# Where the sums, the shared expert and a block's steps stand on the engines of a two-layer model

## The chip, the cores and the metric

One core of a Trainium2 chip runs the whole kernel in one launch. The metric is the device time of one execution in microseconds (us), as the median of several runs. The profiler records one execution apart from these. An instruction belongs to one engine: TensorE (PE in the profile) multiplies matrices, and its weight loads have a lane of their own (PEld); VectorE (DVE), ScalarE (ACT) and GpSimd (POOL) work element by element; SyncE (SP) issues the transfers of the weights.

## The reference, cut to what matters

The model has two layers on 256 tokens of 1024 values. A vector c modulates each layer: the sums below are `silu(c) @ w`.

```python
def ada(c, w, b, n):
    m = jax.nn.silu(c) @ w + b
    return [t[:, None, :] for t in jnp.split(m, n, axis=-1)]

def modulate(h, shift, scale):
    return h * (1 + scale) + shift
...
def moe(h, w_router, e_bias, w_gate, w_up, w_down, ws_gate, ws_up, ws_down):
    ...
    routed = grouped_experts(xt, eidx, w, w_gate, w_up, w_down)
    shared = swiglu(xt, ws_gate, ws_up, ws_down)
    return (routed + shared).reshape(B, S, D)
...
    for i in range(DEPTH):
        sh1, sc1, g1, sh2, sc2, g2 = ada(c, ada_w[i], ada_b[i], 6)
        h = modulate(rmsnorm(x, norm_mix[i]), sh1, sc1)
        if i < N_A_LAYERS:
            y = gmlp_mixer(h, a_w_in[i], a_b_in[i], a_ln_g[i], a_ln_b[i],
                           a_w_s[i], a_b_s[i], a_w_out[i])
        else:
            if kv is None:
                kv = shared_kv(x, c, kv_norm, kv_ada_w, kv_ada_b, kv_w_k, kv_w_v)
            j = i - N_A_LAYERS
            y = moba_mixer(h, b_w_q[j], b_w_o[j], kv[0], kv[1], kv[2])
        x = x + g1 * y
        h = modulate(rmsnorm(x, norm_ffn[i]), sh2, sc2)
        x = x + g2 * moe(h, moe_router[i], moe_bias[i], moe_w_gate[i], moe_w_up[i],
                         moe_w_down[i], sh_w_gate[i], sh_w_up[i], sh_w_down[i])
    return rmsnorm(x, final_norm)
```

Each token goes to 8 of 64 experts, and to the shared expert besides. All inputs are float32.

## The kernel before

All of it lies on one core, in this order: the first eight sums and the norm; the gMLP mixer of layer 0; routing and experts of layer 0; attention of layer 1 with its shared keys and values; routing and experts of layer 1; the final norm.

**Weights.** They arrive in tiles of 1 MB (`w`, 128 partitions x 8 x 256 values) on SP's queue, in the order in which the program fetches them, each as soon as one of 14 places in a pool is free. A place is free once the last instruction that reads its tile is done.

**The mixer and attention** are lists of steps on PE (48 in the mixer: 16 `Tok`, 16 `Feat`, 16 `Out`). `split` prepares the weights of a coming step: `high` casts the tile to a rounded copy on ACT, and `low` writes the difference (`scr<-w,scr`) on DVE, on POOL at every fourth step from 16 to 43 in the mixer; two casts and two low halves are also made before the mixer's first step. Between steps, `tick` takes instructions of the open sums, as many as the table `BUDGET` grants each engine.

**A sum** (class `Sum`, 56 of them) is 256 columns of `silu(c) @ w`: one tile `w`, in which row-block k is scaled by column k of `cs` (silu of c) and the eight blocks are added. Mode "v" does it with 8 instructions on DVE. Mode "q" does it with 8 scalings on ACT and 3 additions on POOL. `lighter` chooses the mode when a sum begins. In both modes `total` then sums over the partitions with two matmuls of one column (`wk<-onesf,w`), and `close` adds the bias into `adaT` or `kvT`.

**The prologue of an expert stage** ranks the experts (`order`), after which SP can fetch experts in that order (experts 0 and 1 are fetched ahead). It places the tokens (`slotT`, `slotU`), works out routing weights (`wsel`, `GT`, `gu`), and runs the whole first half of the shared expert: `shared_up` (32 matmuls of 256 columns) and `shared_act`. `gather` then picks the tokens of the first four blocks (`s` is the selection matrix, built on DVE from `slotU`). `gates` scales the shared expert's last weights.

**The expert stage** runs 55 blocks of up to 128 token places; `ORDER` is the table in which experts, by rank, come to the blocks and their tiles are fetched; -1 in it stands for `shared_down`. On PE a block b is: `gate_up` of b, `scatter` of b-2 (adds results to the output), `share`, `down` of b-1, `flip` (transpose of b's activation), `place`, and `gather` for the next group of four. At block `SHARED_AT`, which follows from the place of -1, comes `shared_down`. A group's selection is prepared by `prep`. Most blocks are narrow: 32 columns of weights in each of four quarters of PE's columns.

Of the kernel before, what the change touches and what calls it, by code (L numbers as in the profile page):

```python
# [33 lines left out]
QUIET = (2, 5)  # L34

# [7 lines left out]
BUDGET = ((1.0, 1.2, 2.5), (1.6, 1.2, 2.5), (0.6, 1.2, 2.5))  # L43
# [11 lines left out]
BUDGET1 = ((1.3, 1.2, 2.5),) * 3 + ((0.8, 0.2, 2),) + ((1.8, 1.6, 3.4),) * 2 + ((1.4, 1.5, 2.5),) * 2  # L55
# [124 lines left out]
def tile_model(ctx: ExitStack, tc: tile.TileContext, A: dict, out: bass.AP):  # L180
# [103 lines left out]
    G.memset(onesf, 1.0)  # L284
    ident = cst.tile([P, P], F32, name="ident")
# [26 lines left out]
    class Sum:  # L312
# [3 lines left out]

        def __init__(self, w, biasT, at, dstT, dst=None, mode="v"):
            self.w, self.biasT, self.at, self.dstT, self.dst, self.mode = w, biasT, at, dstT, dst, mode
            self.ops = {V: [], S: [], G: []}
# [18 lines left out]
        def begin(self):  # L338
            for e in (V, S, G):
                for _, f in self.ops[e]:  # L340
                    f()
                self.ops[e] = []

        def total(self, pt):

            for q in range(2):
                T.matmul(pt[:, q:q + 1], self.w[:, 0, q * P:(q + 1) * P], onesf[:, 0:1], start=True, stop=True)
# [140 lines left out]
    def split(steps, k, pool, turns=None):  # L488
# [17 lines left out]
    credit = {V: 0, S: 0, G: 0}  # L506

    def tick(tv, ts, tg):

        spread()  # L510
        for f in list(active):
            if not f.left(V, S, G):
                f.age = getattr(f, "age", 0) + 1
                if f.age > 2:
                    f.finish()
                    active.remove(f)
        for e, t in ((V, tv), (S, ts), (G, tg)):
            credit[e] = min(credit[e], 0) + t
            for f in active:
                while credit[e] > 0 and f.ops[e] and not (e is G and f.left(V, S)):  # L520
# [4 lines left out]
    def lighter():  # L525

        return "q" if sum(f.left(S) for f in active) < sum(f.left(V) for f in active) + 0.1 else "v"

    def pump(*engs):

        for e in engs:
            for f in active:
                if not (e is G and f.left(V, S)):
# [4 lines left out]
    def settle(n=99):  # L538

        fs = [f for f in active if not f.left(V, S, G)][:n]  # L540
# [68 lines left out]
    def moe(l, own, rw, first, rest):  # L609
# [42 lines left out]
        pump(G)  # L652
# [6 lines left out]
        rest("q")  # L659
# [23 lines left out]
        pump(G)  # L683

# [20 lines left out]
        def gates():  # L705

            for q in range(2):
                S.copy(gq[64 * q:64 * q + 64, :], g2[l][64 * q:64 * q + 64, 512 * q:512 * q + 512])
            for k, eng in enumerate((G, V)):
# [79 lines left out]
        settle()  # L789
        close()  # L790
# [3 lines left out]
        shared_up(16 - SH1)  # L794
        spread()
# [6 lines left out]
        rest(*"vqvqvq")  # L802

        wsel = om([P, 2, NE])
        wsum = om([P, 2], tag="t1", bufs=8)
        for tt in range(2):
            V.scalar_tensor_tensor(wsel[:, tt, :], cr[:, tt, :], -2.5e38, sc[:, tt, :], ALU.is_lt, ALU.mult,
                                   accum_out=wsum[:, tt:tt + 1])
        wrec = om([P, 2], tag="t1", bufs=8)
        V.reciprocal(wrec, wsum)  # L810
        for tt in range(2):
            V.tensor_scalar(wsel[:, tt, :], wsel[:, tt, :], wrec[:, tt:tt + 1], 2.5, ALU.mult, ALU.mult)
        pump(V, S, G)
        ready = all(f.dst is None for f in active)
        if ready:
            gates()
# [3 lines left out]
        settle(1)  # L820
        close()
        shared_up(4)
        pgt = wk((NE, 256))
        for tt in range(2):
            T.transpose(pgt[:, tt * P:(tt + 1) * P], wsel[:, tt, :], ident)
        settle()
        close()
        spread()
        if not ready:
            flush(lambda f: f.dst is not None)  # L830
            gates()
        GT = om([NE, 256], tag="GT", bufs=1)
        S.copy(GT, pgt)
        pgu = wk((P, 2, NU))
        for tt in range(2):
            T.matmul(pgu[:, tt, :], GT[:, tt * P:(tt + 1) * P], puf, start=True, stop=True)
        gu = om([P, 2, NU, 2], F32R, tag="gu", bufs=1)
        V.tensor_copy(gu[:, :, :, 0], pgu)
        V.tensor_tensor(gu[:, :, :, 1], pgu, gu[:, :, :, 0], ALU.subtract)
# [142 lines left out]
        shared_act(0)  # L982
        shared_act(1)
        for c in range(4):
            gather(0, c)
        share(0)
        prep(1)
# [40 lines left out]
        def run():  # L1028
# [7 lines left out]
            for b in range(nblk + 2):  # L1036
                g, j = divmod(b, 4)

                late = b >= nblk - 1
                if b == SHARED_AT:  # L1040
# [12 lines left out]
                if b == nblk - 1:  # L1053
                    ht[b] = flip(hd)
                    scatter(sts.pop(b - 1), ys.pop(b - 1))
                if b == nblk or b >= 1 and not late:
                    y = finish(b - 1)
                if b == nblk + 1:
                    warm(10)
                    scatter(sts.pop(b - 2), ys.pop(b - 2))  # L1060
                if b < nblk:
                    if not late:
                        ht[b] = flip(hd)
                    pp = place(groups[g][1][:, 2 * j:2 * j + 2, :].rearrange("e u i -> e (u i)"))
                    if g + 1 < ng:
# [9 lines left out]
                tick(1.6, 1.6, 4.2)  # L1075
# [63 lines left out]
    with phase("pb") as pool:  # L1139
# [25 lines left out]
        for i in range(8):  # L1165
            f = ada(0, i, load(A["wada"][0, i]), "q" if i in QUIET else "v")
# [28 lines left out]
        for q in range(2):  # L1195
            low(early[q], wi[0][:, 4 * q:4 * q + 4, :], G)
# [100 lines left out]
        for k in range(n + 16):  # L1297
            for at, x in BEGIN:
                if at == k:
                    begin(x, lighter())  # L1300
            if k in (2, 6, 10):
                fetch_bv(512 * (k + 2) // 4, 512)
            split(steps, k, pool, 4 if 16 <= k < 44 else None)
# [23 lines left out]
            tick(*((0, 1.2, 0) if 17 <= k < 20 or k > 45 else BUDGET[k // 16]))  # L1327
# [309 lines left out]
```

## Time and profile before

| | us |
|---|---|
| three runs | 1463.18, 1464.41, 1467.83 |
| median | 1464.41 |
| profiled execution | 1460.32 |
| its span | 1458.6 |
| PE busy in the span | 1352.2 (93%) |
| PE weight loads | 893.6 (61%) |
| DVE busy | 853.3 (58%) |
| ACT busy | 537.5 (37%) |
| POOL busy | 213.9 (15%) |

The profiled execution's own time is 1.7 us above its span. Busy times are those of one execution; matmuls overlap, and their ends are modelled. The trace lists an fp32 matmul of the program as two instructions on PE. The clock granted to TensorE is given as a share of full speed; its mean over the execution is 0.961. The share of transfers is the mean over 16 DMA engines.

### The profile page before, as it was taken

What the parts mean: (1) busy time and instruction counts of PE and PEld (TensorE: products, weight loads), DVE (VectorE), ACT (ScalarE), POOL (GpSimd) and SP (SyncE); (2) the same over time, 40 slices, a digit from 0 to 9 for tenths busy, and PEclk for the clock granted to TensorE, in tenths of its full rate; (3) what the DMA queues carried; (4) which work ended last, traced back from release to release, by engine and by line L of the source; (5) the groups of instructions that cost most, each with busy time, mean ns of one, the idle gap of its engine ahead of it and who ended that gap; (6) DMA issues with size and microseconds to landing.
All of it is one profiled execution on the core that took longest, in us unless ns stands there. A gap on an engine that the chain in (4) does not pass through costs nothing. (4 is left out here: it accounts for less than half of the span.)

```text
span 1458.6 us, 27101 instructions
## 1 busy us (share of the span) xinstructions
PE 1352.2 (93%) x10782; PEld 893.6 (61%) x10782; DVE 853.3 (58%) x1568; ACT 537.5 (37%) x1143; POOL 213.9 (15%) x160
## 2 busy tenths in 40 slices
PE   4797888899999999999988988899999999999996
PEld 3797866655555555555547966775555555555553
DVE  7898897544444444444459977854444444444444
ACT  4565556222322222323236656342322223222222
POOL 4135355110000000000004644320000000000000
PEclk7799999899999999999999989999999999999998
DMA  9876767499999999999995855759999999999995
GB/s 371 323 262 230 271 224 314 173 368 418 420 419 419 419 419 419 420 418 420 419 403 210 324 178 207 286 206 390 405 419 419 420 419 419 419 419 420 419 419 216
DMA packets 72697, 516.59 MB, mean 354 GB/s; under 512 B 8308, under 2 KB 8436, under 8 KB 10358
## 3 DMA queue, kind: packets, MB, share of 16 engines
q1 hardware_dynamic: 72132, 514.03, 87.3%
q8 instruction: 86, 1.41, 0.4%
q10 hardware_dynamic: 436, 0.79, 0.2%
q14 instruction: 43, 0.35, 0.1%
HBM read 513.75 MB, written 1.05 MB: 353 GB/s over the span
## 5 line engine op out<-in xcount | busy, mean ns | idle before, releaser
L194 PE MATMUL wk<-w,b 128*32 128x256 f32 (+1 forms) x4928 | 413.2, 386 | 10.7 <-DMA w<-in_wexp_dram 10.7
L194 PEld LDWEIGHTS wk<-w,b 128*32 128x32 f32 (+1 forms) x4928 | 236.2, 122 | 153.5 <-DMA w<-in_wexp_dram 16.3
L194 DVE TENSOR_TENSOR s<-s,s 64x512 fp32r<-64x512 f32 x220 | 151.0, 686 | 125.3 <-ACT s L194 121.8
L194 PE MATMUL wk<-w,ht 128*32 128x512 f32 (+1 forms) x1232 | 212.5, 601 | 0.4 <-ACT ht L194 0.4
L194 DVE TENSOR_TENSOR s<-wk,g 128x512 f32<-128x512 f32 x110 | 76.1, 692 | 185.2 <-PE wk L194 185.2
L194 POOL TENSOR_TENSOR w<-w 128x1024 f32<-128x1024 f32 (+2 forms) x84 | 135.0, 1608 | 183.1 <-ACT w L194 179.4
L194 DVE SCALAR_TENSOR_TENSOR w<-w,cs 128x256 f32<-128x256 f32 x196 | 153.7, 785 | 5.3
L194 PE MATMUL wk<-s,b 128*128 128x256 f32 (+2 forms) x1024 | 149.4, 295 | 0.0
L194 POOL TENSOR_TENSOR t<-t,mhalf 128x2 f32<-128x2 f32 (+1 forms) x7 | 4.6, 662 | 971.7 <-DVE t L194 971.7
L194 ACT COPY ht<-wk 128x128 f32<-128x128 f32 x110 | 29.3, 266 | 312.0 <-PE wk L194 312.0
L194 ACT CAST s<-s 64x512 fp32r<-64x512 f32 x220 | 134.4, 611 | 15.2 <-DVE s L194 12.4
L194 PEld LDWEIGHTS wk<-s,b 128*128 128x128 f32 (+1 forms) x1024 | 124.7, 185 | 15.7 <-issue 1.1
L194 PE MATMUL acc<-s,h 128*128 128x512 f32 x440 | 131.6, 420 | 0.4 <-DVEq L1086 0.4
L194 ACT ACTIVATE b<-wk,adaT,sc 128x256 f32<-128x256 f32 x112 | 63.3, 565 | 180.5 <-DVE b L194 180.5
L194 DVE TENSOR_SCALAR b<-wk,sc,adaT 128x256 f32<-128x256 f32 x112 | 61.0, 544 | 100.5 <-PE wk L194 100.2
L194 ACT ACTIVATE h<-wk 64x256 f32<-64x256 f32 (+1 forms) x114 | 43.0, 378 | 195.0 <-PE wk L194 195.0
L194 PEld LDWEIGHTS wk<-w,ht 128*32 128x32 f32 (+1 forms) x1232 | 50.4, 120 | 94.3 <-issue 89.3
L194 PEld LDWEIGHTS acc<-s,h 128*128 128x128 f32 x440 | 74.0, 188 | 52.7 <-DVE s L194 35.1
L194 DVE TENSOR_TENSOR scr<-w,scr 128x1024 fp32r<-128x1024 f32 x71 | 102.5, 1449 | 5.8 <-ACT scr L194 5.7
L194 DVE SCALAR_TENSOR_TENSOR h<-wk,ws,h 64x256 f32<-64x256 f32 x110 | 54.0, 491 | 80.1 <-ACT h L194 79.3
L194 ACT CAST scr<-w 128x1024 fp32r<-128x1024 f32 x80 | 83.2, 1045 | 45.8 <-PE wk L194 23.2
L194 ACT ACTIVATE w<-w,cs 128x256 f32<-128x256 f32 x224 | 96.6, 502 | 0.9 <-DMA w<-in_wada_dram 0.8
(238 smaller groups left out, 1428.9 us busy)
## 6 DMA issues: line engine op xcount, KB each, us to landing
w<-in_wexp_dram SPq DMA_DIRECT2D x384, 1024.0 KB, 16.7
w<-in_wada_dram SPq DMA_DIRECT2D x48, 1024.0 KB, 8.0
w<-in_win_dram SPq DMA_DIRECT2D x16, 1024.0 KB, 7.1
w<-in_wqkvo_dram SPq DMA_DIRECT2D x16, 1024.0 KB, 8.6
w<-in_wout_dram SPq DMA_DIRECT2D x8, 1024.0 KB, 6.4
w<-in_wkva_dram SPq DMA_DIRECT2D x8, 1024.0 KB, 6.5
w<-in_wsh_dram SPq DMA_DIRECT2D x6, 1024.0 KB, 4.8
xt<-in_x_dram SPq DMA_DIRECT2D x1, 1024.0 KB, 10.0
```

The lines of the kernel that those rows point to most:

```text
L194: r = f(*a, **k)
```

## The change

A third mode of a sum, "p", takes the place of "q": eight matmuls on PE, each with one column of `cs`, broadcast to 32 columns, as weights and one row-block of `w` (256 columns) moving. Four matmuls of a call go to four quarters of the partitions of one PSUM tile, the second call adds to them. ACT copies the 128x256 result into the tile, and `total` multiplies it with 1/32 instead of 1. The first eight sums all take this mode; later `lighter` takes "v" where DVE has little of sums left, else "p". All low halves go to DVE. In the whole program 39 of 56 sums take mode "p" (8 at the start, 15 in the mixer, 3 in the first prologue, 13 in attention); 17 stay in mode "v" (28 before).

In the prologue, half of `shared_up` and `shared_act` stay ahead of the gather, and the other half is moved into block 2. The routing weights are worked out among the gathers. In a block, `scatter` and `share` stand behind `place`. `ORDER` has other numbers, and `SHARED_AT` goes from 3 to 20.

```diff
-BUDGET = ((1.0, 1.2, 2.5), (1.6, 1.2, 2.5), (0.6, 1.2, 2.5))
+BUDGET = ((1.0, 0.9, 0.9), (1.4, 0.9, 0.9), (0.1, 0.9, 0.9))
...
-BUDGET1 = ((1.3, 1.2, 2.5),) * 3 + ((0.8, 0.2, 2),) + ((1.8, 1.6, 3.4),) * 2 + ((1.4, 1.5, 2.5),) * 2
+BUDGET1 = ((1.5, 0.9, 0.9),) * 8
...
+            if mode == "p":
+                self.ps = None
+                for q in range(2):
+                    self.add(T, 0.45, lambda q=q: self.four(q))
+                self.add(S, 0.4, lambda: S.copy(o, self.ps))
+                return
             for k in range(KT):
                 c = cs[:, k:k + 1]
-                if mode == "q":
-                    self.add(S, 0.4, lambda k=k, c=c: S.activation(w[:, k, :], w[:, k, :], AF.Copy, scale=c))
-                elif k:
-                    self.add(V, 0.4, lambda k=k, c=c: V.scalar_tensor_tensor(o, w[:, k, :], c, o, ALU.mult, ALU.add))
+                if k:
+                    self.add(V, 0.5, lambda k=k, c=c: V.scalar_tensor_tensor(o, w[:, k, :], c, o, ALU.mult, ALU.add))
                 else:
                     self.add(V, 0.4, lambda c=c: V.tensor_scalar(o, o, c, None, ALU.mult))
-            for k, t in ((4, 2.3), (2, 1.2), (1, 0.7)) if mode == "q" else ():
-                self.add(G, t, lambda k=k: G.tensor_tensor(w[:, 0:k, :], w[:, 0:k, :], w[:, k:2 * k, :], ALU.add))
+
+        def four(self, q):
+            if self.ps is None:
+                self.ps = wk((P, 256))
+            for j in range(4):
+                k = 4 * q + j
+                T.matmul(self.ps[32 * j:32 * j + 32, :], cs[:, k:k + 1].to_broadcast([P, 32]), self.w[:, k, :],
+                         start=(q == 0), stop=(q == 1))
...
-    def lighter():
-
-        return "q" if sum(f.left(S) for f in active) < sum(f.left(V) for f in active) + 0.1 else "v"
+    def lighter(v=True):
+
+        return "v" if v and sum(f.left(V) for f in active) < 1 else "p"
...
-            low(f.h, f.part(), G if turns and k % turns == turns - 1 else V)
+            low(f.h, f.part())
...
+        while sums:
+            rest("p")
+            pump(T, S)
+        settle()
+        close()
+        shared_up(6)
+        spread()
         psu = wk((P, 2, NU))
         for tt in range(2):
             T.matmul(psu[:, tt, :], slotT[:, tt * P:(tt + 1) * P], pub, start=True, stop=True)
-        settle(1)
-        close()
-        shared_up(4)
...
-        shared_up(12)
+        shared_up(16 - SH1 - 6)
+        shared_act(0)
         slotU = om([P, 2, NU], tag="slotU", bufs=1)
...
+                if b == 2:
+                    shared_up(16)
+                    shared_act(1)
                 if b == SHARED_AT:
                     shared_down()
...
+                    if b == 0:
+                        share(0)
                     hd = act(pg, groups[g][2][64:128, j // 2, j % 2:j % 2 + 1])
-                if 2 <= b < nblk:
-                    scatter(sts.pop(b - 2), ys.pop(b - 2))
-                if j == 1 and g + 1 < ng:
-                    share(g + 1)
...
                     pp = place(groups[g][1][:, 2 * j:2 * j + 2, :].rearrange("e u i -> e (u i)"))
+                    if b >= 2 and not late:
+                        scatter(sts.pop(b - 2), ys.pop(b - 2))
+                    if j == 1 and g + 1 < ng:
+                        share(g + 1)
                     if g + 1 < ng:
                         gather(g + 1, j)
...
-            f = ada(0, i, load(A["wada"][0, i]), "q" if i in QUIET else "v")
+            f = ada(0, i, load(A["wada"][0, i]), "p")
```

On PE, at the start of the program (numbers are those of tiles: `w` a weight tile, `wk` and `acc` PSUM tiles), the last four of the eight totals stand before alone ahead of the mixer's first matmuls:

```order
L194 MATMUL wk_140<-onesf,w_221 128x1 x2
L194 MATMUL wk_140<-onesf,w_233 128x1 x2
L194 MATMUL wk_140<-onesf,w_245 128x1 x2
L194 MATMUL wk_140<-onesf,w_260 128x1 x2
L194 MATMUL wk_140<-onesf,w_272 128x1 x2
L194 MATMUL acc_445<-scr_286,hh_104 128x256 x2
```

In the changed program the eight matmuls of each sum stand ahead of its total (`c_76` is the column of 1/32):

```order
L192 MATMUL wk_228<-w_226,cs 32x256 x7
L192 MATMUL wk_142<-c_76,w_226 128x1 x2
L192 MATMUL wk_242<-w_240,cs 32x256 x8
L192 MATMUL wk_142<-c_76,w_240 128x1 x2
L192 MATMUL wk_256<-w_254,cs 32x256 x8
L192 MATMUL wk_142<-c_76,w_254 128x1 x2
L192 MATMUL wk_270<-w_268,cs 32x256 x8
L192 MATMUL wk_142<-c_76,w_268 128x1 x2
L192 MATMUL wk_284<-w_282,cs 32x256 x8
L192 MATMUL wk_142<-c_76,w_282 128x1 x2
L192 MATMUL acc_457<-scr_298,hh_106 128x256 x2
```

The sums moved from other engines to PE, one after the other, each followed by its total.

On PE, in the prologue of layer 0, from the middle of `shared_up` (`wk<-b,w`) to the first matmul of `gather` (`wk<-s,b`), before:

```order
L194 MATMUL wk_2294<-b_306_2256,w_424 128x256 x4
L194 LDWEIGHTS slotT_2383
L194 MATMUL wk_2420<-pub_2387,slotT_2383 128x112
L194 LDWEIGHTS slotT_2383
L194 MATMUL wk_2420<-pub_2387,slotT_2383 128x112
L194 MATMUL wk_2423<-onesf,w_430 128x1 x2
L194 MATMUL wk_2427<-b_306_2256,w_422 128x256 x4
L194 MATMUL wk_2432<-ident,sm_2389 64x128 x2
L194 MATMUL wk_2435<-onesf,w_432 128x1 x2
L194 MATMUL wk_2441<-puf_2385,GT_2439 128x112 x2
L194 MATMUL wk_2427<-b_306_2256,w_424 128x256 x4
L194 MATMUL wk_2427<-b_306_2256,w_422 128x256 x4
```

In the changed program, between the same points:

```order
L192 MATMUL wk_2290<-b_329_2255,w_436 128x256 x4
L192 MATMUL wk_2290<-b_329_2255,w_434 128x256 x2
L192 LDWEIGHTS slotT_2362
L192 MATMUL wk_2414<-pub_2366,slotT_2362 128x112
L192 LDWEIGHTS slotT_2362
L192 MATMUL wk_2414<-pub_2366,slotT_2362 128x112
L192 MATMUL wk_2290<-b_329_2255,w_434 128x256 x2
L192 MATMUL wk_2290<-b_329_2255,w_436 128x256 x4
L192 MATMUL wk_2441<-s_370_2428,b_309_2172 128x256
```

The second half (tile `wk_2427` before), the totals and the routing weights' matmuls have left this place.

On DVE, in the same prologue, before (`s_353` is the first selection matrix, `s_313` what `shared_act` writes):

```order
L194 SCALAR_TENSOR_TENSOR w_430<-w_430,cs 128x256 x7
L194 TENSOR_TENSOR w_426<-w_426,g_182_1470 128x1024
L194 TENSOR_TENSOR kvT<-wk_2423,pk 128x2
L194 TENSOR_TENSOR kvT<-wk_2435,pk 128x2
L194 CAST gu_2444<-wk_2441 128x224
L194 TENSOR_TENSOR gu_2444<-wk_2441,gu_2444 128x224
L194 TENSOR_TENSOR slotU_2459<-wk_2420,tab 128x224
L194 TENSOR_TENSOR s_353_2461<-slotU_2459,tab 128x512
L194 TENSOR_SCALAR pu_2463<-tab,rank_2354 64x256
L194 TENSOR_TENSOR s_313_2292<-wk_2294,h_356_2466 128x256
L194 TENSOR_TENSOR s_313_2292<-wk_2427,h_357_2469 128x256
```

In the changed program (`s_370` is the selection, `s_336` the output of `shared_act(0)`):

```order
L192 CAST pub_2366<-puf_2364 64x112
L192 TENSOR_TENSOR kvT<-wk_2398,pk 128x2 x3
L192 TENSOR_TENSOR s_336_2288<-wk_2290,h_368_2423 128x256
L192 TENSOR_TENSOR slotU_2426<-wk_2414,tab 128x224
L192 TENSOR_TENSOR s_370_2428<-slotU_2426,tab 128x512
L192 TENSOR_SCALAR pu_2430<-tab,rank_2350 64x256
```

The sum, the gates' multiply and the routing weights have left the way to `slotU`, and the first half's multiply now stands ahead of it.

## Rows read from the trace of the kernel before

**Rows 1.** Busy time by stage; columns in the first line.

```profile
core 0: us, PE busy (x) PEld busy (x) DVE busy (x) ACT busy (x) POOL busy (x), PEclk, DMA share, GB/s
0.00:47.67 47.67, 19.04 (x84) 15.00 (x85) 35.77 (x62) 17.11 (x35) 17.60 (x22) 0.67 0.95 384
47.67:232.41 184.74, 166.67 (x1147) 156.25 (x1148) 163.75 (x224) 107.88 (x207) 79.10 (x47) 0.94 0.68 250
232.41:284.18 51.77, 41.15 (x230) 34.03 (x228) 35.33 (x93) 24.77 (x53) 20.83 (x15) 0.87 0.71 271
284.18:759.96 475.78, 468.39 (x4032) 262.76 (x4031) 218.61 (x427) 130.81 (x281) 4.34 (x3) 1.00 0.99 409
759.96:930.20 170.24, 148.32 (x1026) 127.52 (x1027) 149.11 (x241) 106.45 (x247) 78.80 (x65) 0.93 0.63 239
930.20:974.64 44.44, 39.86 (x241) 34.64 (x239) 27.60 (x89) 20.37 (x42) 12.51 (x9) 0.92 0.71 284
974.64:1449.70 475.06, 468.80 (x4028) 263.36 (x4027) 218.47 (x425) 127.37 (x273) 0.00 (x0) 0.99 0.97 399
```

**Rows 2.** Timeline at the start: start us, length us, instruction, count, idle before and releaser.

```profile
30.48 1.99 ACT L194 CAST scr<-w 128x1024 fp32r<-128x1024 f32 x2 [4.18 <-DMA w<-in_win_dram]
...
45.08 1.01 PE L194 MATMUL wk<-onesf,w 128*128 128x1 f32 x4 [2.51 <-DVE w L194]
...
47.67 2.56 PE L194 MATMUL acc<-scr,hh 128*128 128x256 f32 x10 [1.58 <-ACT h L194]
```

**Rows 3.** Timeline in the mixer, near 83 and near 120 us.

```profile
83.23 1.01 DVE L194 SCALAR_TENSOR_TENSOR w<-w,cs 128x256 f32<-128x256 f32 x2
...
120.12 7.52 DVE L194 SCALAR_TENSOR_TENSOR w<-w,cs 128x256 f32<-128x256 f32 x4
121.11 3.77 POOL L194 TENSOR_TENSOR w<-w 128x1024 f32<-128x1024 f32 x2 [0.35 <-ACT w L194]
...
129.36 3.30 PE L194 MATMUL wk<-hh,scr 128*128 128x256 f32 x14 [7.56 <-DVE scr L194]
...
131.38 1.22 DVE L194 TENSOR_TENSOR scr<-w,scr 128x1024 fp32r<-128x1024 f32 x1
```

**Rows 4.** Busy time and clock in two stretches of mixer and attention; columns as in rows 1.

```profile
125.70:132.40 6.70, 3.04 (x14) 3.04 (x15) 6.63 (x7) 0.00 (x0) 2.52 (x2) 0.50 0.32 93
846.00:859.40 13.40, 9.57 (x41) 7.82 (x42) 9.99 (x19) 7.33 (x21) 8.11 (x7) 0.50 0.55 191
```

**Rows 5.** Timeline of a narrow block: gather, then gate_up.

```profile
445.90 1.22 PE L194 MATMUL wk<-s,b 128*128 128x256 f32 x8
...
447.05 3.66 PE L194 MATMUL wk<-w,b 128*32 128x256 f32 x64
```

**Rows 6.** Timeline of the prologue of layer 0 and its first block.

```profile
246.21 4.55 POOL L194 TENSOR_TENSOR w<-w 128x1024 f32<-128x1024 f32 x3
...
246.37 2.35 DVE L194 TENSOR_TENSOR sm<-sm,eb 128x128 f32<-128x128 f32 x1
...
256.07 0.21 DVE L194 CAST order<-wk 1x64 int32<-1x64 f32 x1 [0.30 <-PE wk L194]
...
274.62 5.45 PE L194 MATMUL wk<-b,w 128*128 128x256 f32 x24
279.72 4.19 PE L194 MATMUL wk<-s,b 128*128 128x256 f32 x32
...
288.85 0.33 PE L194 MATMUL wk<-ident,h 64*128 64x64 f32 x2 [1.00 <-DVE h L194]
```

**Rows 7.** Timeline of the second routing stretch.

```profile
926.83 4.83 DVE L194 SCALAR_TENSOR_TENSOR w<-w,cs 128x256 f32<-128x256 f32 x3
...
935.65 2.27 PE L194 MATMUL wk<-ident,xt 128*128 128x128 f32 x8 [3.04 <-DVE xt L194]
...
948.64 0.29 DVE L194 TENSOR_TENSOR sm<-sm,eb 128x128 f32<-128x128 f32 x1
```

**Rows 8.** PE's waits in the blocks of layer 0: us in total, times, longest.

```profile
PE wk L194 <- DMA w<-in_wexp_dram: 5.9, 6, 3.4
```

**Rows 9.** PE's waits in attention: us in total, times, longest.

```profile
PE acc L194 <- ACT pm L194: 5.3, 3, 2.6
```

More of the change, by code (lines that the diff above doesn't have):

```diff
@@ L284, in tile_model @@
     G.memset(onesf, 1.0)
+    c32 = cst.tile([P, 1], F32, name="c32")
+    G.memset(c32, 1.0 / 32.0)
     ident = cst.tile([P, P], F32, name="ident")
@@ L346, in total @@
             for q in range(2):
-                T.matmul(pt[:, q:q + 1], self.w[:, 0, q * P:(q + 1) * P], onesf[:, 0:1], start=True, stop=True)
+                T.matmul(pt[:, q:q + 1], self.w[:, 0, q * P:(q + 1) * P], (c32 if self.mode == "p" else onesf)[:, 0:1],
+                         start=True, stop=True)
         def close(self, pt):
@@ L486, in ep, with split @@
                     self.ep_(tt, self.p[tt])
-    def split(steps, k, pool, turns=None):
+    def split(steps, k, pool):
         if k + LA < len(steps):
@@ L504, in begin, with tick @@
         active.append(kvada(x[1], w, mode) if x[0] == "k" else ada(int(x[0] == "A"), x[1], w, mode))
-    credit = {V: 0, S: 0, G: 0}
-    def tick(tv, ts, tg):
+    credit = {V: 0, S: 0, T: 0}
+    def tick(tv, ts, tp):
         spread()
         for f in list(active):
-            if not f.left(V, S, G):
+            if not f.left(V, S, T):
                 f.age = getattr(f, "age", 0) + 1
-                if f.age > 2:
+                if f.age > 1:
                     f.finish()
                     active.remove(f)
-        for e, t in ((V, tv), (S, ts), (G, tg)):
+        for e, t in ((S, ts), (V, tv), (T, tp)):
             credit[e] = min(credit[e], 0) + t
             for f in active:
-                while credit[e] > 0 and f.ops[e] and not (e is G and f.left(V, S)):
+                while credit[e] > 0 and f.ops[e] and not (e is S and f.left(T)):
                     t, op = f.ops[e].pop(0)
@@ L532, in pump @@
             for f in active:
-                if not (e is G and f.left(V, S)):
+                if not (e is S and f.left(T)):
                     for _, op in f.ops[e]:
@@ L538, in settle @@
     def settle(n=99):
-        fs = [f for f in active if not f.left(V, S, G)][:n]
+        fs = [f for f in active if not f.left(V, S, T)][:n]
         if fs:
@@ L651, in moe @@
         early = len(active)
-        pump(G)
+        pump(T, V)
         squares(0, 2)
@@ L801, in moe @@
         V.tensor_copy(pub, puf)
[L802 to L816, printed above, removed]
+        pump(S)
+        while sums:
[5 more added lines that the diff above has]
+        spread()
         psu = wk((P, 2, NU))
@@ L981, in moe @@
         prep(0)
-        shared_act(0)
-        shared_act(1)
-        for c in range(4):
-            gather(0, c)
-        share(0)
-        prep(1)
+        wsel = om([P, 2, NE])
+        wsum = om([P, 2], tag="t1", bufs=8)
+        for tt in range(2):
+            V.scalar_tensor_tensor(wsel[:, tt, :], cr[:, tt, :], -2.5e38, sc[:, tt, :], ALU.is_lt, ALU.mult,
+                                   accum_out=wsum[:, tt:tt + 1])
+        wrec = om([P, 2], tag="t1", bufs=8)
+        V.reciprocal(wrec, wsum)
+        for tt in range(2):
+            V.tensor_scalar(wsel[:, tt, :], wsel[:, tt, :], wrec[:, tt:tt + 1], 2.5, ALU.mult, ALU.mult)
+        for c in range(3):
+            gather(0, c)
+        pgt = wk((NE, 256))
+        for tt in range(2):
+            T.transpose(pgt[:, tt * P:(tt + 1) * P], wsel[:, tt, :], ident)
+        GT = om([NE, 256], tag="GT", bufs=1)
+        S.copy(GT, pgt)
+        gather(0, 3)
+        pgu = wk((P, 2, NU))
+        for tt in range(2):
+            T.matmul(pgu[:, tt, :], GT[:, tt * P:(tt + 1) * P], puf, start=True, stop=True)
+        gu = om([P, 2, NU, 2], F32R, tag="gu", bufs=1)
+        V.tensor_copy(gu[:, :, :, 0], pgu)
+        V.tensor_tensor(gu[:, :, :, 1], pgu, gu[:, :, :, 0], ALU.subtract)
+        flush(lambda f: f.dst is not None)
+        halfgates()
         found = []
@@ L1299, in tile_model @@
                 if at == k:
-                    begin(x, lighter())
+                    begin(x, lighter(k < 30))
             if k in (2, 6, 10):
                 fetch_bv(512 * (k + 2) // 4, 512)
-            split(steps, k, pool, 4 if 16 <= k < 44 else None)
+            split(steps, k, pool)
             e = k + 4 - n
```

58 lines of the change are left out of this document (21 added, 37 removed), and 6 rows, old and new, of the table ORDER.

## Prediction

> **What bounds the kernel now.** I began with busy time by stage [rows 1]: the start, the gMLP mixer, the first routing stretch with its prologue, the expert blocks of layer 0, attention, the second routing stretch, and the blocks of layer 1. Subtract PE's busy time from each length. In the two block stages little is left: in the first, PE is busy 468.39 of 475.78 us and the DMA share is 0.99, so two resources fill it at once. Elsewhere PE idles 28.6 us of the start, 18.1 of the mixer, 10.6 of the first routing stretch, 21.9 of attention and 4.6 of the second routing stretch, and its clock is below 1.00 in each. The time to be had lies there; work put into the block stages is paid for.
>
> Next the single instructions. At the start [rows 2] PE begins the mixer at 47.67 and the last pair of totals at 45.08, after a wait for DVE, while the first mixer tile had landed by 30.48. Sums on DVE and POOL, not transfers, set the start. In the mixer [rows 3], two multiply-adds of a sum take 1.01 us; four take 7.52 us when POOL's adds of another sum run beside them. The low half of the next weights stands behind these on DVE, and PE waits 7.56 us for it. In the stretch of that wait the clock is 0.50 [rows 4].
>
> **The change part by part.** *A sum on TensorE.* It is 8 matmuls of 32x256 in four column quarters; the trace lists an fp32 matmul as two instructions, so 16. The kernel before has none on a sum, but the gate_up of a narrow block has the same shape [rows 5]: 64 instructions are busy 3.66 us, so 16 take 0.9. To this comes the switch between full and quarter columns. Eight gather matmuls ahead of that gate_up take 1.15 us start to start (445.90 to 447.05), where 32 in a row take 4.19 us, 1.05 for eight [rows 6]: 0.1 for one switch, and I take 0.3 for a sum with both ends and its two calls, 1.2 us in all. ACT's copy of the result is off PE's path as long as other steps stand between sum and totals, as they do. The bounds are 0.9 and, if the columns don't overlap, 3.6 (16 at 5.45/24 us, as full-width fp32 matmuls of 256 columns take [rows 6]).
>
> The Trainium skill, TensorEngine Tiling (Array Packing), Key Properties, says that a change of tiling mode, not merely of tile, drains TensorE. It speaks against this change, since every sum enters and leaves the quarter mode; the page gives no time for a drain. The 0.1 us agrees with a small one; without it the 28 sums of mixer and attention would cost 25 us, with my 0.3 they cost 34.
>
> *The start.* Eight sums leave DVE, ACT and POOL. A 1 MB tile takes 2.6 us at the 409 GB/s of the block stage [rows 1], so the last tile of a sum, just ahead of the mixer's on the same queue, lands near 27.9. Then come its sum at about half clock (1.8), ACT's copy (about 0.4) and what followed the last pair before: totals, adaT, scale and h, 2.6 us from 45.08 to 47.67 [rows 2]. That gives 32.7. The other branch is 30.48, two ACT casts of 1.99 together, and DVE's low half at 1.22 [rows 3]: 33.7. With hand-offs I take 34.9: **-12.8**. Bounds: 33.7 (-14), and 39 (-9) if sums queue for the wk banks.
>
> *The mixer.* 15 sums go to TensorE, 6 stay on DVE; POOL's adds and its low halves go, and the locks with them; the seven or so low halves that move to DVE cost it 1.22 us each [rows 3], beside work of PE. The gain is 18.1 us of idle time and of slow clock about 5: the clock's shortfall is 0.06 of 184.74 us, 11.1, and PE works in 3.04 of 6.70 us of such a stretch [rows 4], 0.45 of the time. Against it stand 15 x 1.2 = 18.0, all on PE, which is the bound once the waits are gone, and about 2 of waits that stay (first tile, norm). 23.1 - 20.0: **-3.1**. Bounds: -9.6 (0.9 a sum, no waits left), and +8 if half the stalls and slow stretches stay.
>
> *The first routing stretch.* Before, the table of expert order is read at 256.07, and the first gate_up of a block starts at 284.18 [rows 6]: 28.1 us. After, between them stand three sums (2.7 and 0.3), their totals (1.0), 12 matmuls of the shared expert, 24 instructions (5.45), the gather (4.19), some 1.7 of small routing matmuls, and a new wait, about 2: the multiply of shared_act(0) now precedes slotU on DVE, and waits for an activation; behind slotU are queued the selection matrices s, for which the gather on PE waits. Sum 17.3, 10.8 less. The path to the order loses what POOL does to DVE: 2.35 us for an add [rows 6] that takes 0.29 in layer 1, where POOL has no such work [rows 7], 2.1. Together 12.9; part of it is at low clock in either kernel: **-12**. Bounds: -14 and -8.
>
> *The blocks of layer 0.* shared_up(16) comes in at b == 2: 32 instructions at 5.45/24, 7.3 us of PE. The cover is PE's waits for expert tiles, 5.9 us in six [rows 8], of which I let half count since transfers too have less of a start: **+4**. If all counts it is +1.5. If the shared expert's weights, held longer in the pool (to b == 2, and w2 to b == 20 instead of 3), delay two expert tiles by 2.6 us each, it is 7.3 + 5.2, +12. The other order within a block I cost at nothing: flip needs the activation, which lagged gate_up by 1.00 us where nothing stood between [rows 6], and down of the block before still stands there as cover. Without it the wait would return in 54 blocks, 54 us. That the experts come in another order moves loads, not bytes. The gates' multiplies of w2 on DVE and POOL move behind the first block and stay hidden, since shared_down, which needs them, comes only at b == 20; at b == 3, as before, three blocks would cover them.
>
> *Attention.* 21.9 us idle, of which some 5 belong to the residual and norm at its head; 16.7 remain. The shortfall of clock is 0.07 of 170.24, 11.9; in its longest slow stretch PE works in 9.57 of 13.40 us [rows 4], 0.7, and I count 7.8 (two thirds). Against 24.5 stand 13 sums, 15.6, and 4 for waits that are ACT's softmax, not sums: ACT's pm accounts for 5.3 us [rows 9]. **-4.9**. Bounds: -13 and +7.
>
> *The second routing stretch.* Three multiply-adds that take 4.83 us on DVE stand ahead of the residual, and PE then waits 3.04 us for xt [rows 7]; I count 3.5 with the slow clock after it. Half the shared expert leaves, 7.3, less about 1 for the new wait: 6.3. **-10**, bounds -12 and -6. Its blocks: **+4** as in layer 0.
>
> The sum is -12.8 - 3.1 - 12 + 4 - 4.9 - 10 + 4 = -34.8. The profiled execution took 1460.32 us, so 1425.5; the median of the runs shown, 1464.41, lies 4.1 above it. Forecast **1429 us**. All lower bounds together make -59.6 (1405), all upper ones +16 (1480); they will hardly all fall on one side.
>
> **The rivals.** *A, slower: the quarters don't overlap.* The place is PE in the mixer and attention. A sum would cost 3.6 + 0.3, so 28 of them add 2.7 x 28 = 76, the three of the prologue 8, and at the start eight sums at half clock, 7 us each, outlast their tiles and put the mixer near 66 instead of 34.9, +31: 1429 + 115 = 1544. It decides from 1.2 + 35/31 = 2.3 us a sum. Against it: rows 5, where quarters that read different operands do overlap. A drain of over a microsecond at every sum would come to the same.
>
> *B, a smaller gain.* The waits change owner: a sum's tile is held until PE, ACT's copy and the totals are done; ACT's pm stays in attention; each block stage pays 12. For it: the DMA share of 0.99 in the blocks, and that PE's extra work there has half its cover by my choice. Blocks +16, and a sixth of the 34.8 us that the mixer and attention idle kept, +6: about 1451.
>
> *C, a larger gain.* No stall of attention and mixer is left (6), a sum costs 0.9 (8), blocks +1.5 each (5): 1410. For it: DVE has far less to do once POOL is off its back.
>
> *D, no change:* the gains of the routing stretches are paid back wholly in the blocks because expert tiles bound them. It would need the start's gain to vanish as well, and nothing waits long for a tile there; about 1464.
>
> **How the numbers follow.** Forecast 0.48, B 0.24, C 0.20, D 0.03, A 0.05. The forecast's own range is 1418 to 1440; taking in C and most of B, 1404 to 1453 leaves out about 2 in 10. Faster by over 0.3% (4.4 us, about what a measurement of this kernel can tell) 0.92, within it 0.03, slower 0.05.
>
> **What would show it.** The mixer should start near 35; no wait of PE for DVE's low halves over 2 us; 16 instructions of a sum within 1.3 us; the first gate_up 37 to 41 us after the mixer's end; blocks of 477 to 482 us a layer, with shared_up's 32 instructions in the third block. The prediction is wrong if a sum takes over 2 us, if PE still waits 10 us for scr, or if the blocks take 488 or more.

## The result and the profile after

The median went from 1463.80 us (4 runs, 1462.35 to 1467.83) to 1419.76 (4 runs, 1415.02 to 1422.27): ratio 0.969 [0.966, 0.973], 44 us faster. The profiled execution took 1417.81 us. The forecast was 1429 in 1404 to 1453. The busy time by stage, with the same seven stages and the tail (columns as in [rows 1]):

```profile
0.00:46.07 46.07, 32.26 (x213) 19.82 (x213) 5.48 (x19) 12.89 (x27) 3.40 (x15) 0.94 0.94 382
46.07:225.07 179.00, 177.28 (x1394) 157.51 (x1395) 116.57 (x207) 76.74 (x126) 6.08 (x5) 0.99 0.74 273
225.07:264.73 39.66, 33.87 (x234) 26.79 (x232) 21.41 (x79) 18.09 (x38) 10.32 (x7) 0.91 0.68 266
264.73:741.31 476.58, 466.04 (x4068) 273.19 (x4067) 224.21 (x438) 128.37 (x276) 0.00 (x0) 0.99 0.98 411
741.31:899.87 158.56, 153.98 (x1247) 128.01 (x1248) 110.38 (x231) 76.64 (x174) 25.58 (x33) 0.98 0.70 267
899.87:933.18 33.31, 28.48 (x194) 24.16 (x192) 21.35 (x78) 18.25 (x38) 10.36 (x7) 1.00 0.68 271
933.18:1406.57 473.39, 464.73 (x4064) 272.73 (x4063) 220.59 (x428) 128.35 (x276) 0.00 (x0) 0.99 0.97 404
1406.57:1416.10 9.53, 0.00 (x0) 0.00 (x0) 4.62 (x11) 2.71 (x6) 0.69 (x1) 0.62 0.29 111
```

Set against [rows 1], stage by stage, with the term of the forecast:

| stage | before | after | change | forecast |
|---|---|---|---|---|
| start | 47.67 | 46.07 | -1.6 | -12.8 |
| mixer | 184.74 | 179.00 | -5.7 | -3.1 |
| first routing stretch | 51.77 | 39.66 | -12.1 | -12 |
| blocks of layer 0 | 475.78 | 476.58 | +0.8 | +4 |
| attention | 170.24 | 158.56 | -11.7 | -4.9 |
| second routing stretch | 44.44 | 33.31 | -11.1 | -10 |
| blocks of layer 1 | 475.06 | 473.39 | -1.7 | +4 |

The sum is right to 8 us, but the start misses by 11 the one way, attention by 7 and the blocks by 9 the other. PE's idle time in the mixer fell from 18.1 to 1.7 us and in attention from 21.9 to 4.6. The transfer rate in the blocks (second part of the page, 40 slices of the span) rose too, from 419 to 426 GB/s, which nothing in the forecast explains. First the kernel before, then the changed one:

```profile
GB/s 371 323 262 230 271 224 314 173 368 418 420 419 419 419 419 419 420 418 420 419 403 210 324 178 207 286 206 390 405 419 419 420 419 419 419 419 420 419 419 216
```

```profile
GB/s 371 340 272 300 297 233 252 176 404 425 426 425 426 425 426 425 427 424 427 425 404 269 358 246 231 187 273 415 420 425 425 426 426 426 425 426 425 426 425 209
```

Of the signs that the prediction named, one failed: the mixer started at 46.07, not near 35. A sum's 16 instructions took 1.07 us, PE waited for DVE's low halves 0.7 us, the first gate_up came 39.7 us after the mixer's end, and the blocks took 476.6 and 473.4 us, just under the 477 to 482 named.

The experiments ask what the sums brought alone, what the moved parts brought, where the rate came from, what a sum costs, and why the start gained so little.

### The profile page after: what moved, and what is told of

Its sections match the earlier page's. It is cut to its first block, busy times and chain, and to the rows that moved or that the text cites. A ratio compares the mean times of both kernels' runs of the same rounds, so it can differ in the third digit from the quotient of the medians.

```text
span 1416.1 us, 27976 instructions
## 1 busy us (share of the span) xinstructions
PE 1356.6 (96%) x11406; PEld 902.2 (64%) x11406; DVE 724.6 (51%) x1489; ACT 462.0 (33%) x958; POOL 56.4 (4%) x68
## 5 line engine op out<-in xcount | busy, mean ns | idle before, releaser
L192 PE MATMUL wk<-w,b 128*32 128x256 f32 (+1 forms) x4928 | 414.1, 387 | 15.3 <-DMA w<-in_wexp_dram 15.3
L192 PE MATMUL wk<-s,b 128*128 128x256 f32 (+2 forms) x1024 | 142.9, 289 | 4.6 <-DVE s L192 4.6
L192 PEld LDWEIGHTS wk<-s,b 128*128 128x128 f32 (+1 forms) x1024 | 132.5, 188 | 15.6 <-issue 5.6
L192 ACT CAST s<-s 64x512 fp32r<-64x512 f32 x220 | 134.4, 611 | 15.6 <-DVE s L192 12.9
L192 PEld LDWEIGHTS wk<-w,ht 128*32 128x32 f32 (+1 forms) x1232 | 54.3, 121 | 97.8 <-issue 89.5
L192 DVE TENSOR_TENSOR scr<-w,scr 128x1024 fp32r<-128x1024 f32 x80 | 99.3, 1247 | 4.9 <-ACT scr L192 4.7
L192 PEld LDWEIGHTS wk<-ident,h 64*128 64x128 f32 (+1 forms) x226 | 22.5, 137 | 91.6 <-DVE h L192 91.1
L192 PE MATMUL wk<-hh,scr 128*128 128x256 f32 x576 | 73.8, 286 | 0.0
L192 PEld LDWEIGHTS wk<-hh,scr 128*128 128x128 f32 x576 | 70.2, 192 | 3.3 <-issue 3.3
L192 DVE SCALAR_TENSOR_TENSOR w<-w,cs 128x256 f32<-128x256 f32 x119 | 58.6, 493 | 2.9
```

The source lines that it names most:

```text
L192: r = f(*a, **k)
```

## The experiments

**The sums without the moves.** The changed kernel, with prologue, blocks and table put back:

```diff
-        while sums:
-            rest("p")
-            pump(T, S)
+        rest(*"pppppp")
...
-        shared_up(16 - SH1 - 6)
-        shared_act(0)
+        shared_up(12)
```

> Only the sums change (with their budgets, and the low halves on DVE); prologue, block order and table are those of before. If the sums bring what the stages of the two profiles show (start -1.6, mixer -5.7, attention -11.7, and about 3 to 4 in each routing stretch by freeing DVE of POOL), the time is 25 to 28 us below before, ratio 0.981 to 0.984, with mixer and attention each as short as in the full change. Rival: the sums gain little by themselves because the blocks wait for tiles; then 0.99 or above.

Measured 1417.14 us, 0.969 [0.966, 0.972]: all of the gain, and more than the 25 to 28 us expected. Mixer and attention were as short as after the full change, 179.2 and 156.9 us. The two routing stretches took 43.9 and 38.5, 7.9 and 5.9 less than before. But the blocks, in which nothing was changed, were shorter too:

```profile
268.90:741.00 472.10, 467.20 (x4032) 262.67 (x4031) 221.94 (x435) 127.40 (x273) 0.00 (x0) 1.00 0.99 413
...
936.40:1405.70 469.30, 464.76 (x4028) 261.20 (x4027) 218.33 (x425) 127.37 (x273) 0.00 (x0) 1.00 0.97 404
```

They lost 3.7 and 5.8 us; their mean rates are 413 and 404 GB/s, where before had 409 and 399.

**The moves without the sums.** The kernel before, with prologue, blocks and table of the change:

```diff
-        shared_up(12)
+        shared_up(16 - SH1 - 6)
+        shared_act(0)
...
+                if b == 2:
+                    shared_up(16)
+                    shared_act(1)
```

> The sums stay in the modes of before; only the prologue, the block order and the table change. Expected from the stages: 8 to 9 us less in the first prologue, 6 to 8 in the second, and 0 to +4 in each block stage: ratio 0.990 to 0.995. Mixer and attention as before. Rival: blocks bound by tiles give the prologue's gain back, ratio 0.997 to 1.003.

Measured 1469.68 us, 1.004 [1.002, 1.006]: 6 us slower. In size that is the rival, and a little beyond. In layer 0 it is not the rival's mechanism, for the prologue gained nothing that could be given back: from the expert order to the first block it takes 28.3 us against 28.1 before, because PE waits there for a sum on DVE:

```profile
266.12 1.87 PE L194 MATMUL wk<-onesf,w 128*128 128x1 f32 x8 [9.01 <-DVE w L194]
```

In layer 1, which has no sums there, it takes 16.3 against 20.3, and the blocks give more than that back: they take 484.7 and 480.9 us, 8.9 and 5.9 more than before. PE's waits for expert tiles, over the whole span, first this kernel, then the kernel before (us, times, longest):

```profile
PE wk L194 <- DMA w<-in_wexp_dram: 25.0, 9, 5.4
```

```profile
PE wk L194 <- DMA w<-in_wexp_dram: 10.7, 9, 3.4
```

PE's busy time in the blocks hardly changed (470.3 and 465.7 us, before 468.4 and 468.8). The waits grew by 14.3 us, nearly all of the 14.8 that the blocks lost.

**The table put back.**

```diff
-    1, 50, 35, 22, 49, 11, 27, 33, 0, 46, 20, 34, 58, 4, 19, 63, 56, 32, 38, 7, 31, 26, 29, 47, -1, 3, 17, 48,
+    0, 63, 21, -1, 52, 56, 1, 32, 7, 46, 43, 36, 45, 6, 25, 23, 44, 15, 20, 26, 27, 30, 51, 8, 11, 50, 28, 41,
...
```

> The full change with the old table of experts (shared_down at block 3 again). My forecast costed the table at nothing: within 2 us of the full change, ratio 0.967 to 0.971. Rival: the new table gives tiles their places earlier or takes longer to release the shared expert's last tile; then the blocks differ by 4 us or more a layer, in waits for expert tiles.

Measured 1422.61 us, 0.973 [0.970, 0.976]. The blocks took 480.1 and 476.5 us, 3.5 and 3.1 more than in the full change; the interval overlaps that of the full change, so the run by itself does not separate them, and the table is worth at most some 3 us a layer.

**The block order put back.**

```diff
+                if b >= 2 and not late:
+                    scatter(sts.pop(b - 2), ys.pop(b - 2))
+                if j == 1 and g + 1 < ng:
+                    share(g + 1)
                 if late:
```

> The full change with scatter and share ahead of down, flip and place again. Costed at nothing: within 2 us of the full change. Rival: a wait of about 1 us a block appears for flip or for down, 20 us or more slower.

Measured 1420.07 us, 0.970 [0.966, 0.974]: no difference. Yet the order does change PE's work. A block between two gate_up of 64 columns, half of PE's, in this kernel:

```profile
446.16 3.67 PE L192 MATMUL wk<-w,b 128*64 128x256 f32 x32
449.77 1.20 PE L192 MATMUL acc<-s,h 128*128 128x512 f32 x4
450.90 1.92 PE L192 MATMUL wk<-w,ht 128*32 128x512 f32 x16
...
454.39 3.67 PE L192 MATMUL wk<-w,b 128*64 128x256 f32 x32
```

and the same block in the full change:

```profile
445.96 3.67 PE L192 MATMUL wk<-w,b 128*64 128x256 f32 x32
449.56 1.92 PE L192 MATMUL wk<-w,ht 128*32 128x512 f32 x16
...
451.91 1.20 PE L192 MATMUL acc<-s,h 128*128 128x512 f32 x4
452.94 1.12 PE L192 MATMUL wk<-s,b 128*128 128x256 f32 x8
453.99 3.67 PE L192 MATMUL wk<-w,b 128*64 128x256 f32 x32
```

From one gate_up to the next it is 8.23 us against 8.03. With scatter next to gather, PE changes between full and part width two times fewer in a block: 0.1 us a change, as [rows 5, 6] had it. Over a layer's blocks PE is busy 474.2 and 472.7 us in this kernel and 466.0 and 464.7 in the full change, some 8 us less. It does not appear in the run's time. PE waits for tiles instead: 2.8 us in all here, 15.3 in the full change.

**The address alone.** The change's constant of 1/32 takes 32 bytes of each partition, so every tile allocated behind it moves. The kernel before with an unused one:

```diff
     G.memset(onesf, 1.0)
+    pad = cst.tile([P, 1], F32, name="pad")
+    G.memset(pad, 1.0)
```

> The kernel before with an unused tile of one column among the constants, nothing else: every later tile moves by 32 bytes, as the column of 1/32 moves it in the change. Theory: the address sets the transfer rate of the blocks (419 GB/s in the profiles of before and of moves_only, 425 to 426 in those with the tile of 1/32). Then the rate is 425 to 426 here, the block stages are 3 to 6 us shorter each, ratio 0.993 to 0.996. Rival: the rate comes from the engines' work (POOL's adds, DVE) or from the day's chip; then 419 and ratio 0.998 to 1.002.

Measured 1450.80 us, 0.991 [0.989, 0.993]: 13 us faster from an unused column. The rate, by slices of the span:

```profile
GB/s 371 322 261 200 279 251 318 181 315 424 426 426 425 426 426 425 426 425 425 426 411 206 345 155 190 330 204 357 408 425 426 425 426 426 425 425 425 425 426 223
```

and by windows, the blocks of layer 0 and of layer 1:

```profile
286.50:756.20 469.70, 465.78 (x4032) 261.51 (x4031) 218.59 (x427) 130.79 (x281) 4.35 (x3) 1.00 0.99 414
971.20:1439.80 468.60, 464.46 (x4028) 261.27 (x4027) 218.46 (x425) 127.37 (x273) 0.00 (x0) 1.00 0.97 404
```

Each stage of blocks is some 6 us shorter than in [rows 1], with the work unchanged.

**The change without the shift.** 1/32 in a spare column of another constant:

```diff
-    c32 = cst.tile([P, 1], F32, name="c32")
...
-    mhalf = cst.tile([P, 2], F32, name="mhalf")
+    mh = cst.tile([P, 3], F32, name="mh")
+    mhalf = mh[:, 0:2]
+    c32 = mh[:, 2:3]
```

> The full change with the 1/32 kept in a spare column of another constant, so that the weight tiles lie where they lay before. By the theory of the address the rate falls to 419 GB/s, each block stage is 6 to 8 us longer, 1430 to 1434 us, ratio 0.977 to 0.981. Rival: same as the full change, 0.967 to 0.971.

Measured 1432.48 us, 0.978 [0.976, 0.980], as expected: the blocks take 484.0 and 480.9 us at 419 GB/s. So some 13 us of the result's 44 are the address, in either kernel.

**The other five places.** The expert stage's own five places in the pool lie behind other tiles; an unused column ahead of them moves them and none of the nine:

```diff
+    pad = sb.tile([P, 1], F32, tag="pad", name="pad", bufs=1)
+    G.memset(pad, 1.0)
     onesf = cst.tile([P, P], F32, name="onesf")
```

In the full change:

> The full change with another unused column ahead of the five places of the expert stage's own pool, so that all 14 places begin at a multiple of 64 bytes (before 5 of 14 did, in the change 9). Two shares and two rates give 2.40 us for an aligned tile and 2.56 for the others, so 436 GB/s here; PE's waits for tiles in the blocks, 15.3 us in both, mostly go: 10 to 14 us below the full change, ratio 0.958 to 0.962. Rival: rate unchanged, same time as the full change.

In the kernel before:

> The kernel before with the unused column ahead of the expert stage's own five places only, so that all 14 places lie 32 bytes off a multiple of 64. Runs so far: nine off and five on 419 GB/s, nine on and five off 426, all on 426. If the nine alone decide, 419 GB/s here and the time of before; if the sum of places counts, less, 410 to 416, and blocks some 5 us longer.

The first: 1419.95 us, 0.970 [0.968, 0.972], 426 GB/s, the time of the full change. My theory of multiples of 64 bytes fell. The second, in a single run: 1465.04 us, 419 GB/s. So the address of the five places does not count. What counts is that of the other nine, or of something else that only the column among the constants moves, such as the activations' tiles allocated behind the nine; no run parts these. The nine lie 224 bytes past a multiple of 256 in the kernels with 419 GB/s, and on a multiple of 256 in those with 426; the five lay 64, 96 or 128 past one in all of these runs. The Trainium skill, DMA: Bandwidth & Descriptors, How a descriptor splits into AXI transactions, says that when a descriptor does not begin at a multiple of 256 bytes, its first transaction begins at the boundary below, and that the unused bytes in front cost time too. The nine places agree with that, the five do not. In the trace of the full change 98% of the 8 KB packets that start between 300 and 700 us take 309 ns, although 5 of the 14 places lie off such a multiple; in the trace of before only 14.5% do, fewer than the share of the five places, and the mean is 316. That speaks against a price paid tile by tile, and why the rate changes stays open. That the five places on such a multiple would bring more was not tried.

**A sum computed twice.** All but the first eight on TensorE:

```diff
-                for q in range(2):
-                    self.add(T, 0.45, lambda q=q: self.four(q))
+                for q in (0, 1, 0, 1) if self.twice else (0, 1):
+                    self.add(T, 0.225 if self.twice else 0.45, lambda q=q: self.four(q))
```

> The full change, each sum on TensorE after the first eight computed twice over (the second time overwrites the first; same budget a step). 31 sums more: at 0.9 to 1.0 us each, as the rows of a sum show, 28 to 31 us slower than the full change, ratio 0.988 to 0.991. Rival: idle time of PE or the blocks' waits hide part; then under 20 us. If the switch of column width cost 0.3 us at each sum it is not doubled here, so only the matmuls show.

Measured 1444.16 us, 0.987 [0.985, 0.989], 24 us more than the full change and less than the 28 to 31 expected. The mixer took 192.1 us, 12.9 more for 15 sums, and attention 169.8, 11.1 more for 13: 0.86 us a sum, nearly all of the 0.93 that the rows show for one of two (1.86 us for the pair). The three sums of the first prologue, which stand behind the expert order, hardly show: from the order to the end of the blocks it is 498.4 us, in the full change 497.1.

**A sum at full width.** The quarters given up:

```diff
-                T.matmul(self.ps[32 * j:32 * j + 32, :], cs[:, k:k + 1].to_broadcast([P, 32]), self.w[:, k, :],
-                         start=(q == 0), stop=(q == 1))
+                T.matmul(self.ps, cs[:, k:k + 1].to_broadcast([P, P]), self.w[:, k, :],
+                         start=(k == 0), stop=(k == KT - 1))
```

> The full change with each sum's 8 matmuls at full width (128 columns, 1/128 in the totals), all into one place, so nothing overlaps and the column width never changes. If four quarters overlap as the gate_up rows say, a sum takes 3.6 instead of 1.0 us: 28 x 2.6 in mixer and attention, 8 in the prologue, 15 to 25 at the start, some 95 to 105 us slower than the full change, 1515 to 1525. Rival: the switch of column width costs much of what the overlap gains; then under 50 us slower.

Measured 1497.43 us (median of 2), 1.023 [1.019, 1.028]: slower than before, 78 us more than the full change, less than the 95 to 105 expected. Mixer +32.2, attention +28.9, first routing stretch +8.7, start +8.7 us. A sum at full width, then one in quarters in the full change, each from its start to that of the next row:

```profile
913.65 3.70 PE L192 MATMUL wk<-w,cs 128*128 128x256 f32 x16
917.00 1.18 PE L192 MATMUL wk<-hh,scr 128*128 128x256 f32 x7
```

```profile
885.90 1.07 PE L192 MATMUL wk<-w,cs 128*32 128x256 f32 x16
886.90 3.06 PE L192 MATMUL acc<-scr,b 128*128 128x512 f32 x12
```

3.35 us against 1.00, both changes of width included.

**The start.** Its rows in the full change:

```profile
10.51 7.19 PE L192 MATMUL wk<-w,w 2*128 2x128 f32 x32
17.62 1.94 PE L192 MATMUL wk<-w,cs 128*32 128x256 f32 x16
20.05 1.01 PE L192 MATMUL wk<-c,w 128*128 128x1 f32 x4 [0.49 <-ACT w L192]
...
35.74 1.07 PE L192 MATMUL wk<-w,cs 128*32 128x256 f32 x16
37.30 0.61 PE L192 MATMUL wk<-c,w 128*128 128x1 f32 x4 [0.49 <-ACT w L192]
37.84 1.07 PE L192 MATMUL wk<-w,cs 128*32 128x256 f32 x16
```

The sums stand in PE's queue behind the layer norm's matmuls (32 instructions) and the transposes of x, and each total waits 0.49 us for ACT's copy with nothing between. One sum takes 2.10 us from start to start (35.74 to 37.84), and none of the last ones waits for its tile, which I had as the bound. So:

```diff
-            f = ada(0, i, load(A["wada"][0, i]), "p")
+            f = ada(0, i, load(A["wada"][0, i]), "v" if i in (0, 2, 4) else "p")
...
             f.begin()
-            f.total(pa[:, 2 * i:2 * i + 2])
+            if i:
+                g.total(pa[:, 2 * i - 2:2 * i])
+            g = f
+            if i == 7:
+                f.total(pa[:, 14:16])
```

> The full change, but of the first eight sums numbers 0, 2 and 4 stay on DVE, which is idle there, and each pair of totals is issued one sum later, so that PE does not wait for ACT's copy. Theory: at the start PE's queue is the bound (eight sums of 2.1 us one after another, behind the layer norm's matmuls and the transposes); the mixer then starts at 36 to 39 instead of 46, 6 to 9 us less, ratio 0.963 to 0.966. Rival: the start is bound by tiles or by the casts, gain below 2 us.

Measured 1410.78 us, 0.963 [0.961, 0.965], 9 us below the full change and the fastest of all. The mixer starts at 37.0:

```profile
33.08 1.01 PE L192 MATMUL wk<-c,w 128*128 128x1 f32 x4 [0.49 <-ACT w L192]
37.00 0.58 PE L192 MATMUL acc<-scr,hh 128*128 128x256 f32 x1 [2.91 <-DVE hh L192]
```

Not all of that is the edit. A part of the 46.07 of the full change was one execution's clock: the kernel with the old table has the same start, its 32 instructions of the layer norm took 4.08 us instead of 7.19, and its mixer started at 40.6. The trace of the old table has the granted clock at 1.00 from 10.7 to 14.1 us; that of the full change has no record of it before 29.9, so the 0.94 of the table by stage says little of the start. Of the seven profiles with the full change's start, two begin the mixer at 40.6 or 40.7 and five at 44.0 to 47.0. In start_mix the 30 of those instructions that the row shows took 4.19 us, so it is to be held against 40.6, and 3.6 us of the 9 are seen in the start; the rest is not located. The two edits of this run were not tried apart.

**The sums alone with that start.** Both edits together:

```diff
-            f = ada(0, i, load(A["wada"][0, i]), "p")
+            f = ada(0, i, load(A["wada"][0, i]), "v" if i in (0, 2, 4) else "p")
...
-        shared_up(16 - SH1 - 6)
-        shared_act(0)
+        shared_up(12)
```

> The sums alone (prologue, block order and table of before) with the start of start_mix. If the moved parts bring nothing on balance, as sums_only and the full change say, this equals start_mix or is 1 to 4 us below it: 1406 to 1411, ratio 0.960 to 0.964.

Measured 1415.23 us, 0.966 [0.963, 0.969], with runs from 1408.84 to 1419.34. Above what was expected, and its interval overlaps that of the sums alone and of the start alone: inconclusive.

## Why the prediction came out as it did

**The sums** were rightly at the centre, and their price was mis-sized on the safe side: 1.00 us instead of 1.2, 0.1 instead of 0.3 for the switches (0.2 x 28, 5.6 us). Without the shift, sums and moves bring 31 us (after_nopad); with the shift in both, the sums bring 34 (before_pad to sums_only). **Attention** was short by 7 because I let 4 us stay for ACT's softmax (pm) and counted a fifth of a microsecond too much for each sum; the wait for pm went as well. PE's waits in attention after:

```profile
PE wk L192 <- POOL t L192: 1.7, 1, 1.7
PE wk L192 <- ACT xt L192: 0.9, 2, 0.8
PE wk L192 <- POOL b L192: 0.9, 3, 0.3
```

ACT had 88 scalings of sums fewer there, with 13 copies in their place, and POOL was busy 25.58 us beside DVE instead of 78.80, so what looked like the softmax's own length [rows 9] was work queued ahead of it; that is the reading of the rows, and no run took pm's wait away by itself.

**The start** is the step that failed. "Then come its sum at about half clock (1.8), ACT's copy (about 0.4) and what followed the last pair before" counts one sum after the last tile. PE's queue held all eight, one after another, behind other work, and ACT's copy was not "off PE's path", since nothing stood between a sum and its totals. start_mix shows it: with three sums on DVE and the totals a sum later, the mixer starts at 37.0, near the 34.9 of the forecast, where the unchanged start at a like clock gave 40.6. The other 5.4 us of the 11 that were missed are the clock of that execution.

**The routing stretches** came out as forecast, -12.1 and -11.1, the first by luck: ahead of the expert order 4.5 us went where I had 2.1, and behind it 7.6 where I had 10.8. The new wait for the selection is there at the 2 us I gave it:

```profile
258.02 4.59 PE L192 MATMUL wk<-s,b 128*128 128x256 f32 x24 [2.05 <-DVE s L192]
```

But only a part of that counts. **The blocks** end at a nearly fixed time after the expert order is known, not after their first gate_up. Where DVE writes the order (same instruction as at 256.07 in [rows 6]), and where the blocks of layer 0 end, in the kernels at 426 GB/s:

| kernel | order | end of blocks | between |
|---|---|---|---|
| before_pad | 258.4 | 756.2 | 497.9 |
| sums_only | 244.1 | 741.0 | 496.9 |
| full change | 244.3 | 741.3 | 497.1 |
| old_block | 243.5 | 742.0 | 498.5 |
| all_64 | 239.1 | 737.5 | 498.4 |

Here the first block starts between 20 and 28 us after the order, PE is busy 8 us more or less in the blocks, and the distance stays within 2 us. The other kernels at 426 GB/s need 498.4 to 500.5 us, but sum_full 507.8: its three sums at full width, 8.7 us more behind the order, do lengthen it. In layer 1 the rule is looser: all ten need 487.1 to 493.1 us, while the first block starts 13.7 to 21.9 us after the order; the two that start at 13.7 need 487.1 and 489.5, those at 19.0 to 21.9 need 488.3 to 491.3. At 419 GB/s it is 503.9 before, 504.5 in after_nopad, 507.5 in before_both and 513.0 in moves_only; the last two are not explained.

The order is needed to fetch the tiles, but they do not flow from there on. SP's fetches of expert tiles behind the order, in the full change and then in the sums alone:

```profile
245.55 6.10 SPq L249 DMA_DIRECT2D w<-in_wexp_dram  x4
275.94 28.09 SPq L249 DMA_DIRECT2D w<-in_wexp_dram  x15
```

```profile
245.34 19.77 SPq L249 DMA_DIRECT2D w<-in_wexp_dram  x6
277.14 31.34 SPq L249 DMA_DIRECT2D w<-in_wexp_dram  x14
```

In between SP waits for PE to free places, in the full change up to 23.0 us at once (window 235 to 310 us):

```profile
SPq L249 <- PE wk L192: 43.5, 10, 23.0
```

So the fetches go on at nearly the same time in both, after two tiles fewer in the full change, although its first block starts 4.1 us earlier. By the program, the moved half of shared_up keeps the shared expert's tiles in their places until block 2, which the prediction had only as a bound ("held longer in the pool"); no run moved it alone.

The sums gain in the routing stretches because they bring the order forward; what the moves take out behind the order, 4.2 and 5.2 us of the two stretches (sums_only to the full change), returns in the blocks as waits for tiles, +4.5 and +4.1. My rival B held that tiles bind, yet I had priced it as 12 us a stage; and D's "paid back wholly in the blocks" is what happened to the moves, not to the sums. The +4 for the blocks was too low for the moves (+6.9 and +4.8 from before_pad), and was hidden by -6 from the address, which no reason of mine contained. Of the 44 us some 13 came from there, about as much as the start's miss took away. The total was right in part by luck, with a partly wrong account.

**Rival A** is measured by sum_full: 78 us over the full change, not 115, since a sum at full width takes 3.35 us where I had 3.9, and the start lost 9 us instead of 31. Its point of decision, 2.3 us a sum, lies between the two kernels, one 44 us faster and the other 34 slower than before.

## What to carry to other kernels

Ask of a stage that two resources fill what its loads need before they can go on: here the list that names them, and free places. What was shortened behind the list was no gain here; what brought the list forward was, to within some 4 us a layer. A small matrix-vector product belongs on TensorE in column quarters when the element engines hold up other work, but only with other matmuls between its parts, since each hand-off to another engine stands in TensorE's queue. Before crediting a change, repeat the kernel before with the change's shift of addresses alone.

## What was not expected of the hardware

An unused column of 4 bytes among the constants made the kernel 13 us faster: transfers in the blocks went from 419 to 426 GB/s when every tile behind it moved by 32 bytes, nine places of the weights from 224 bytes past a multiple of 256 to a multiple of 256 among them. A change between full and part width on TensorE costs 0.1 us (8.23 against 8.03 us a block, two changes fewer). On DVE, the multiply-adds of the sums in the mixer took 825 ns each on average before and 482 after. In the trace of before, the 43 that no work of POOL overlapped took 482 ns, and the 20 that POOL's adds overlapped 1.56 us on average. Before, then after:

```profile
L194 DVE SCALAR_TENSOR_TENSOR w<-w,cs 128x256 f32<-128x256 f32 x63 | 51.9, 825 | 1.6
```

```profile
L192 DVE SCALAR_TENSOR_TENSOR w<-w,cs 128x256 f32<-128x256 f32 x42 | 20.2, 482 | 1.0
```
